# One order of work for the blocks of an expert, lists chosen by masks, at most three blocks unrolled

## The chip, the cores and the metric

The kernel runs on one core of a Trainium2 chip. The metric is the device time of one execution in microseconds (us). Before the change three runs gave a median of 1856.02 us, from 1854.19 to 1857.72. The trace that is read here is one profiled execution of 1859.71 us; the span of its instructions is 1857.6 us.

## What is computed

A decoder layer on 2048 tokens of width 1024 in float32: a mixer (a state-space branch and a convolution branch, gated and projected), a layer norm, a mixture of experts, a layer norm. Only the mixture matters here. Each token is sent to one of 4 groups and to 2 of the 8 experts in that group, 32 experts in all. The rows of an expert are worked in blocks of 128:

```python
def expert_block(args):
    idx, e = args
    xb = xt[idx]
    hid = jax.nn.silu(xb @ w_gate[e]) * (xb @ w_up[e])
    return hid @ w_down[e]
...
y = jax.ops.segment_sum(y_buf.reshape(n_rows, d) * w_buf[:, None], tok_buf, num_segments=n_tok)
```

With the reference's inputs the 32 experts get 11 to 286 rows: 18 experts have one block, 11 have two, 3 have three, 49 blocks together. In order of the experts the blocks are 1 1 1 1 2 1 2 1 2 2 2 1 3 3 2 2 1 1 2 2 1 1 3 1 1 1 2 2 1 1 1 1.

## The kernel before

The mixer and the routing fill the first 1276 us and do not change. Routing writes a table td in DRAM with, for each expert and block, 128 token numbers and weights; cnt holds the counts. The expert stage follows, then the last layer norm on VectorE (from 1798 us on).

Weights are float32 and are split in two parts each, a rounded high part (ScalarE, high) and the rest (VectorE, low); egu holds gate and up of an expert, edn its down matrix. A matmul of float32 precision is three matmuls: high by high, high by low, low by high. Pieces 0 to 3 of an expert's weights are egu, 4 and 5 are edn. The weights of the next expert are split while the present one is multiplied; load and load2 are the DMAs that bring raw weights three experts ahead, on SP's queue.

A block of 128 tokens goes through these steps. gather (Pool, an indirect DMA) brings its rows to a tile. turn transposes them on TensorE in eight pieces (pt), which ScalarE and VectorE split into BH and BL. gateup is 24 matmuls into pg. act makes HID (silu on ScalarE, a product on VectorE). turnh transposes HID in two pieces (ph), split into HH and HL. down is 12 matmuls into pd. emit scales pd by the weights into yy (ScalarE, two halves) and adds it to acc by an indirect DMA of Pool, the scatter. A block is thus 46 matmuls and transposes on TensorE.

On TensorE the steps of neighbouring blocks are interleaved: gateup of a block, turn of the next block, down of the block before, turnh of this block, gateup of the next one. How many blocks an expert has is known only at run time. table(e) loads the count into a register of TensorE, ScalarE, VectorE and Pool (L1369), and each engine branches on it. unit(e, b) is a nest four deep (JB = 4): if the expert has a further block, that block's turn, down, emit, turnh and the next unit follow; if not, the Else holds over(), a copy of the turn of the next expert's first block and the down. So each level has an Else of its own, and an expert of one block jumps over the taken sides of all levels (L1465). The loop over the experts is unrolled.

The rows of a next expert's first block go to XA (two buffers, gathered two experts ahead), those of second and third blocks to XE and XC (gathered by extra, one expert ahead). Which list the last block of an expert has depends on its count; ends copies it by up to four small VectorE copies into IXL and IXQ. BH, BL, HH, HL and HID have two buffers each. Per engine the instructions run in the order of the program; nothing else sets it. After the last expert a count above JB blocks would be worked by a loop (L1524), which does not run here.

Of the kernel before, what the change touches and what calls it, by code (L numbers as in the profile page):

```python
# [10 lines left out]
F32 = mybir.dt.float32  # L11
F32R = mybir.dt.float32r
# [10 lines left out]
S = 2048  # L23
D = 1024
# [4 lines left out]
ALPHA = 2.0 ** 0.25  # L29
EPS = 1e-5  # L30
CAP = 2048
JB = 4
MAGIC = 12582912.0
RSQ = float(0x5F3759DF)

# [50 lines left out]
def layer(ctx, tc, a, out, dbg=None):  # L86
# [1165 lines left out]
    def step(i, *ks):  # L1252
        for k in ks:
            high(i, k)
            low(i, k)
# [6 lines left out]
    for p in range(NP):  # L1262
# [47 lines left out]
        if p == NP - 3:  # L1310
# [27 lines left out]

    ex = ExitStack()
    ep = ex.enter_context(tc.tile_pool(name="ep", bufs=1, side="right"))  # L1340
    XA, XE = [[ep.tile([128, D], F32, name=f"{n}{i}") for i in range(2)] for n in ("xa", "xe")]
    XC = [ep.tile([128, D], F32, name="xc0"),
          wp.tile([128, D], F32, name="xc1", tag="raw", bufs=1, padded_shape=[128, 1024])]
    zero = ident[:, 0:1].to_broadcast([128, D])
    for t in XA:
        A.activation(t, zero, AF.Copy, scale=0.0)
    high(0, 4, 5)
    for t in XE + XC:
        A.activation(t, zero, AF.Copy, scale=0.0)
    high(1, 0, 1)  # L1350

    def pairs(n, name, shape, dt=F32):
        return [ep.tile(shape, dt, name=f"{name}{i}") for i in range(n)]

    BH, BL = [[wp.tile([128, 8, 128], F32R, name=f"{nm}{i}", tag=tag, bufs=2) for i in range(2)]
              for nm, tag in (("bh", "hi"), ("bl", "lo"))]
    HH = pairs(2, "hh", [128, 2, 128], F32R)
    HL = pairs(2, "hl", [128, 2, 128], F32R)
    HID = pairs(2, "hid", [128, FF])
    TAB = ep.tile([128, NE, JB, 2], I32, name="tab")  # L1360
    IXL = pairs(3, "ixl", [128, 2], I32)
    IXQ = pairs(3, "ixq", [128, 2], I32)

    ENG = [ET.PE, ET.Activation, ET.DVE, ET.Pool]
    ALL = ENG + [ET.SP]
    CNT, IX = {}, {}

    def table(e):
        CNT[e] = nc.values_load(cnt[0:1, e:e + 1], engines=ENG, min_val=0, max_val=S)  # L1369
        IX[e] = TAB[:, e]  # L1370

    def lists(e, n):
        A.dma_start(TAB[:, e:e + n].rearrange("p e b c -> p e (b c)"), dap(td, 32 * e, [[1024, 128], [32, n], [1, 2 * JB]]))

    def ends(e, b):

        for t, r in ((IXL[e % 3], IX[e][:, b]), (IXQ[e % 3], IX[e][:, b - 1] if b else IXL[(e - 1) % 3])):
            V.tensor_copy(t[:, 0:1], r[:, 0:1])
            V.tensor_copy(t[:, 1:2].bitcast(F32), r[:, 1:2].bitcast(F32))
            if not e:  # L1380
                break
# [8 lines left out]
    PT = [paux([128, 4, 128], f"pt{i}") for i in range(2)]  # L1390
    PH = paux([128, 2, 128], "ph")

    def turn(xb, i):
        for b in range(2):
            for k in range(4):
                PE.transpose(PT[b][:, k, :], xb[:, (4 * b + k) * 128:(4 * b + k + 1) * 128], ident)
            hi = BH[i][:, 4 * b:4 * b + 4, :]
            A.activation(hi, PT[b], AF.Copy)
            V.tensor_tensor(BL[i][:, 4 * b:4 * b + 4, :], PT[b], hi.bitcast(F32), op=OP.subtract)

    def gateup(i, gu):
        p, hi, lo = PG[i], BH[i], BL[i]
        for k in range(8):
            t = gu[k // 4]
            PE.matmul(p, hi[:, k, :], t[:, 0, k % 4, :], start=k == 0, stop=False)
            PE.matmul(p, hi[:, k, :], t[:, 1, k % 4, :], start=False, stop=False)
            PE.matmul(p, lo[:, k, :], t[:, 0, k % 4, :], start=False, stop=k == 7)

    def act(i, j):
        A.activation(HID[j], PG[i][:, 0:FF], AF.Silu)  # L1410
        V.tensor_tensor(HID[j], HID[j], PG[i][:, FF:2 * FF], op=OP.mult)

    def turnh(j):
        for k in range(2):
            PE.transpose(PH[:, k, :], HID[j][:, 128 * k:128 * k + 128], ident)
        A.activation(HH[j], PH, AF.Copy)  # L1416
        V.tensor_tensor(HL[j], PH, HH[j].bitcast(F32), op=OP.subtract)

    def down(j):
        hh, hl, dn = HH[j], HL[j], DN[j]  # L1420
        for h in range(2):
            c = slice(512 * h, 512 * h + 512)
            for k in range(2):
                PE.matmul(PD[h], hh[:, k, :], dn[:, 0, k, c], start=k == 0, stop=False)
                PE.matmul(PD[h], hh[:, k, :], dn[:, 1, k, c], start=False, stop=False)
                PE.matmul(PD[h], hl[:, k, :], dn[:, 0, k, c], start=False, stop=k == 1)

    def emit(ixc):
        y = ep.tile([128, D], F32, name="yy", bufs=2)
        for h in range(2):  # L1430
            A.activation(y[:, 512 * h:512 * h + 512], PD[h], AF.Copy, scale=ixc[:, 1:2].bitcast(F32))
        G.indirect_dma_start(out=acc, out_offset=bass.IndirectOffsetOnAxis(ap=ixc[:, 0:1], axis=0),
                             in_=y, in_offset=None, bounds_check=S - 1, oob_is_err=False, compute_op=OP.add)

    def unit(e, b):

        i, j = (e + b) % 2, e % 2
        gateup(i, GU[j])
        more = b == 0 and 0 < e < NE - 1
        if more:  # L1440
            step(1 - j, 0, 1, 2)
            high(1 - j, 3)
        if b == 1 and JB > 3:
            with tc.If(CNT[e] > 384):
                gather(XE[j], IX[e][:, 3, 0:1])
        act(i, j)
        if more:
            low(1 - j, 3)
            if e + 3 < NE:
                load(e + 3, 1 - j)  # L1450
        jp, ixp = (j, IX[e][:, b - 1, :]) if b else (1 - j, None)

        def over():
            ends(e, b)
            if e + 1 < NE:
                turn(XA[1 - j], 1 - j)
            if e or b:
                down(jp)
            if b and not e:
                emit(ixp)  # L1460

        if b + 1 == JB:
            over()
            return
        with tc.If(CNT[e] > 128 * (b + 1)) as c:  # L1465
            turn((XE[j], XC[j], XE[j])[b], 1 - i)
            if e or b:
                down(jp)
                emit(ixp if b else IXL[(e - 1) % 3])
            turnh(j)  # L1470
            unit(e, b + 1)
        with c.Else():
            over()

    def extra(e):
        with tc.If(CNT[e] > 128):
            gather(XE[e % 2], IX[e][:, 1, 0:1])
            with tc.If(CNT[e] > 256):
                gather(XC[e % 2], IX[e][:, 2, 0:1])


    low(0, 4, 5)
    load2(2, 0)
    lists(0, 2)
    lists(2, NE - 2)
    high(1, 2, 3, 4, 5)
    low(1, *range(6))
    for e in range(3):
        table(e)
    load(3, 1)  # L1490
    load2(3, 1)
    gather(XA[0], IX[0][:, 0, 0:1])
    gather(XA[1], IX[1][:, 0, 0:1])
    extra(0)
    turn(XA[0], 0)
    for e in range(NE):
        j = e % 2
        if e + 3 < NE:
            table(e + 3)
        if e + 2 < NE:  # L1500
            gather(XA[j], IX[e + 2][:, 0, 0:1])
        if e + 1 < NE:
            extra(e + 1)
        unit(e, 0)
        ahead_ = 0 < e < NE - 1
        if ahead_:
            high(1 - j, 4, 5)
            low(1 - j, 4)
        turnh(j)
        if ahead_:  # L1510
            low(1 - j, 5)
            if e + 3 < NE:
                load2(e + 3, 1 - j)
        if e:
            emit(IXQ[e % 3])
    down((NE - 1) % 2)
    emit(IXL[(NE - 1) % 3])
# [7 lines left out]
    with tc.If(mx > 128 * JB):  # L1525
        with tc.For_i(0, NE, 1) as e:
            c = nc.values_load(cnt[0:1, ds(e, 1)], engines=ALL, min_val=0, max_val=S)
            with tc.If(c > 128 * JB):
                load(e, 0)
                load2(e, 0)  # L1530
                step(0, *range(6))
                with tc.For_i(JB, S // 128, 1) as b:
                    with tc.If(c > b * 128):
                        ix = ep.tile([128, 2], I32, name="ixo", bufs=1)
                        SP.dma_start(ix, td.rearrange("(p e b) c -> e b p c", e=NE, b=S // 128)[ds(e, 1), ds(b, 1)]
                                     .rearrange("e b p c -> p (e b c)"))
                        gather(XA[0], ix[:, 0:1])
                        turn(XA[0], 0)
                        gateup(0, GU[0])
                        act(0, 0)  # L1540
                        turnh(0)
                        down(0)
                        emit(ix)
    ex.close()


# [130 lines left out]
```

## Time and profile before

| What | us |
| --- | --- |
| Median of three runs | 1856.02 |
| Profiled execution | 1859.71 |
| Its span | 1857.6 |
| Expert stage, first gate-up to end of last down | 507.3 |
| TensorE busy in the span | 1712.9 (92%) |
| VectorE busy in the span | 1321.3 (71%) |
| ScalarE busy in the span | 692.6 (37%) |
| Pool busy in the span | 301.1 (16%) |

A row of the timeline gives the start, the length, the engine, the operation with its output and inputs, how many there are, and in brackets how long the engine had been idle and what released it; "issue" means that nothing in the profile explains the wait. Matmuls overlap their neighbours, so a row's length is more than the distance to the next one. The sequencer's rows (a q behind the engine; TensorE's are under PEldq) are register loads, branches and events; they are not counted as busy.

### The profile page before, as it was taken

To read this page: it belongs to the slowest core of one execution; us is meant where nothing else is said; L and a number is where in the kernel's file an instruction comes from. 1 tells how busy PE (TensorE), PEld (TensorE's weight loads), DVE (VectorE), ACT (ScalarE), POOL (GpSimd) and SP (SyncE) were. 2 spreads that over 40 slices of the span, in tenths; PEclk is the share of its full clock that TensorE was granted. 3 is DMA by queue.
4 is the path that set the end of the run, shared out by engine and by line. 5 is a ranking of instruction groups with operands and counts; after the bars stand their busy time and mean duration, and the time that the engine had idled before them with its cause. 6 is when DMAs were issued, how large, how long until landed. Compare 5 with 4: busy or idle time off the path is not lost. (4 is left out here: it accounts for less than half of the span.)

```text
span 1857.6 us, 24068 instructions
## 1 busy us (share of the span) xinstructions
PE 1712.9 (92%) x8360; PEld 1376.4 (74%) x8361; DVE 1321.3 (71%) x2528; ACT 692.6 (37%) x1069; POOL 301.1 (16%) x318
## 2 busy tenths in 40 slices
PE   8999999999999999999999999974899998999940
PEld 7888877777777777877888888853677787877730
DVE  5798787687877884765576678885665556657748
ACT  5111222222222223533321122235665556657744
POOL 2000001101110110000000012212333332323215
PEclk9999999999999999999999999987999999999975
DMA  6321432432342336433553323456888878789755
GB/s 217 92 91 47 121 75 76 141 97 84 97 144 79 97 98 222 121 108 110 185 184 118 143 91 125 171 190 211 266 264 256 269 204 265 220 251 322 231 176 232
DMA packets 213924, 301.40 MB, mean 162 GB/s; under 512 B 29246, under 2 KB 159376, under 8 KB 211168
## 3 DMA queue, kind: packets, MB, share of 16 engines
q1 hardware_dynamic: 166496, 213.32, 35.4%
q0 software_dynamic: 23008, 56.06, 10.9%
q10 hardware_dynamic: 24224, 29.50, 4.7%
q8 instruction: 112, 1.84, 0.4%
q14 instruction: 84, 0.69, 0.1%
HBM read 224.28 MB, written 92.31 MB: 170 GB/s over the span
## 5 line engine op out<-in xcount | busy, mean ns | idle before, releaser
L66 PE MATMUL mm<-xh,whi 128*128 128x512 f32 x896 | 360.8, 403 | 0.0
L66 PE MATMUL mm<-xl,whi 128*128 128x512 f32 x896 | 353.5, 395 | 0.0
L66 PE MATMUL mm<-xh,wlo 128*128 128x512 f32 x896 | 352.2, 393 | 0.0
L66 DVE SCALAR_TENSOR_TENSOR cvw<-cvw,cw 128x1024 f32<-128x1024 f32 x240 | 292.1, 1280 | 0.0
L66 PE MATMUL pg<-egu,bh 128*128 128x512 f32 x784 | 251.5, 402 | 4.7 <-ACT hh L1416 2.8
L66 PEld LDWEIGHTS mm<-xh,whi 128*128 128x128 f32 x896 | 168.3, 188 | 47.9 <-ACT y L712 5.8
L66 PEld LDWEIGHTS mm<-xh,wlo 128*128 128x128 f32 x896 | 168.2, 188 | 41.4
L66 PEld LDWEIGHTS mm<-xl,whi 128*128 128x128 f32 x896 | 168.6, 188 | 36.4 <-issue 0.2
L66 DVE TENSOR_TENSOR egu<-eraw,egu 128x1024 fp32r<-128x1024 f32 x128 | 150.8, 1220 | 33.9 <-ACT egu L1245 33.9
L66 PEld LDWEIGHTS pg<-egu,bh 128*128 128x128 f32 x784 | 145.3, 190 | 37.6 <-ACT hh L1416 3.3
L66 PE MATMUL mm<-yt,whi 128*128 128x512 f32 x512 | 163.8, 401 | 2.0 <-ACT yt L858 1.5
L66 PE MATMUL mm<-wo,mh 128*128 128x512 f32 x512 | 163.6, 401 | 0.0
L66 PE MATMUL pg<-egu,bl 128*128 128x512 f32 x392 | 156.1, 398 | 1.1 <-DVE bl L66 1.1
L731 ACT ACTIVATE gt<-mm,cols 128x512 f32<-128x512 f32 x64 | 44.0, 687 | 265.5 <-PE mm L66 265.5
L66 PE MATMUL pd<-edn,hh 128*128 128x512 f32 x392 | 131.3, 416 | 11.3 <-issue 9.4
L1245 ACT ACTIVATE egu<-eraw 128x1024 fp32r<-128x1024 f32 x128 | 124.9, 1058 | 0.2 <-issue 0.2
L66 PEld LDWEIGHTS mm<-yt,whi 128*128 128x128 f32 x512 | 96.7, 190 | 26.0 <-ACT yt L858 1.5
L66 PEld LDWEIGHTS mm<-wo,mh 128*128 128x128 f32 x512 | 95.0, 190 | 21.8 <-issue 1.2
L66 DVE TENSOR_TENSOR edn<-erd,edn 128x1024 fp32r<-128x1024 f32 x64 | 77.9, 1219 | 38.8 <-ACT edn L1245 38.6
L66 PE MATMUL mm<-yt,wlo 128*128 128x512 f32 x256 | 101.7, 397 | 0.0
L66 PE MATMUL mm<-wo,ml 128*128 128x512 f32 x256 | 101.7, 397 | 0.0
L66 PEld LDWEIGHTS pd<-edn,hh 128*128 128x128 f32 x392 | 72.5, 195 | 27.4 <-issue 11.4
(287 smaller groups left out, 2646.3 us busy)
## 6 DMA issues: line engine op xcount, KB each, us to landing
eraw<-in_w_gate_dram SPq DMA_DIRECT2D x64, 512.0 KB
eraw<-in_w_up_dram SPq DMA_DIRECT2D x64, 512.0 KB
erd<-in_w_down_dram SPq DMA_DIRECT2D x32, 1024.0 KB
gd<-gt ACTq DMA_DIRECT2D x64, 256.0 KB
gl<-gd SPq DMA_DIRECT2D x64, 256.0 KB
wraw<-in_w_in_dram SPq DMA_DIRECT2D x28, 512.0 KB
xt<-in_x_dram SPq DMA_DIRECT2D x16, 512.0 KB
rg<-in_x_dram SPq DMA_DIRECT2D x8, 1024.0 KB
```

Of the source, the lines that this page charges most:

```text
L66: return f(*args, **kw)
L731: A.activation(gt, p, AF.Sigmoid, bias=cols[:, BI + 12 + m:BI + 13 + m])
L1245: A.activation(h, src, AF.Copy)
```

## The change

All blocks follow one order now: gateup and act of a block, turn of the next rows, down of the block before, emit of that block. An expert's first block is outside the If; further(e, b) is one nest of Ifs without Else for the second and third block (JB = 3). For the turn to be the same whatever comes next, select builds two tables once, by masks from the counts (MK: block b exists; OH: block b is the last): NX[e, b] is the list that follows block b of expert e, either of the same expert or the first of the next, LL[e] is list and weights of the last block of e. Where block b is the last, XN holds the next expert's rows. Otherwise XN holds the second block's rows, X1 the third's or the next expert's, X2 the next expert's. XN is gathered one expert ahead, X1 and X2 at the start of the same expert. There is one tile B for both parts of the turned rows, one HH, HL and HID. The copies of ends are gone. emit of the last block stands before the splitting of the next edn (high 4, 5), and those stand before the Ifs.

```diff
-JB = 4
+JB = 3
...
+    for b in range(JB):
+        V.tensor_scalar(MK[:, :, b], pc, 128.0 * b, None, op0=OP.is_gt)
+    V.memset(MK[:, :, 0:1], 1.0)
+    V.tensor_tensor(OH[:, :, 0:JB - 1], MK[:, :, 0:JB - 1], MK[:, :, 1:JB], op=OP.subtract)
+    V.tensor_copy(OH[:, :, JB - 1:JB], MK[:, :, JB - 1:JB])
...
+    def select():
+
+        V.tensor_copy(TF[:, 0:NE], TAB[:, :, :, 0])
+        V.memset(TF[:, NE:NE + 1], float(1 << 20))
+        first = TF[:, 1:NE + 1, 0:1]
+        t = LP[:, :, 0:JB - 1, 0]
+        V.tensor_tensor(t, TF[:, 0:NE, 1:JB], first.to_broadcast([128, NE, JB - 1]), op=OP.subtract)
+        V.tensor_tensor(t, t, MK[:, :, 1:JB], op=OP.mult)
+        V.tensor_tensor(NX[:, :, 0:JB - 1], t, first.to_broadcast([128, NE, JB - 1]), op=OP.add)
+        V.tensor_copy(NX[:, :, JB - 1:JB], first)
+        V.tensor_tensor(LP[:, :, :, 0], TF[:, 0:NE], OH, op=OP.mult)
+        V.tensor_tensor(LP[:, :, :, 1], TAB[:, :, :, 1].bitcast(F32), OH, op=OP.mult)
+        lf = TF[:, 0:NE, 0:2]
+        V.tensor_reduce(lf, LP.rearrange("p e b c -> p e c b"), axis=AX.X, op=OP.add)
+        V.tensor_copy(LL[:, :, 0], lf[:, :, 0])
+        V.tensor_copy(LL[:, :, 1].bitcast(F32), lf[:, :, 1])
...
-    def ends(e, b):
-
-        for t, r in ((IXL[e % 3], IX[e][:, b]), (IXQ[e % 3], IX[e][:, b - 1] if b else IXL[(e - 1) % 3])):
-            V.tensor_copy(t[:, 0:1], r[:, 0:1])
-            V.tensor_copy(t[:, 1:2].bitcast(F32), r[:, 1:2].bitcast(F32))
...
+    def further(e, b):
+
+        j = e % 2
+        with tc.If(CNT[e] > 128 * b):
+            turnh()
+            block(e, b, (e + b) % 2, GU[j])
+            if e + 1 < NE or b + 1 < JB:
+                turn(XB[b])
+            down(j)
+            emit(TAB[:, e, b - 1, 0:1], TAB[:, e, b - 1, 1:2])
+            if b + 1 < JB:
+                further(e, b + 1)
...
+        if e + 2 < NE:
+            table(e + 2)
+        if e + 1 < NE:
+            gather(XN[1 - j], NX[:, e + 1, 0:1])
+        with tc.If(CNT[e] > 128):
+            gather(X1, NX[:, e, 1:2])
...
+        turn(XN[j])
+        if e:
+            down(1 - j)
+            emit_last(e - 1)
+        if more:
+            high(1 - j, 4, 5)
+            low(1 - j, 4)
+        further(e, 1)
+        turnh()
```

TensorE at the end of an expert, before the change: the end of the last Else copy of the down (pd), the branch out of the If, turnh (ph), the load of a count, and the branch for the gathers.

```order
L66 MATMUL pd1_10182<-edn0_10152,hh0_10166 128x512 x2
L66 MATMUL pd1_10182<-edn0_10152,hl0_10168 128x512
L1465 UNCONDITIONAL_BRANCH
L66 MATMUL ph_10185<-ident_69,hid1_10171 128x128 [waits DVE_49]
L66 MATMUL ph_10185<-ident_69,hid1_10171 128x128
L1369 TENSOR_LOAD cnt_5895
L1369 ISA x2
L1476 COMPARE_AND_BRANCH
```

The same place after it, where the matmuls belong to the third block and the two branches with a wait are the skipped sides of the two Ifs.

```order
L66 MATMUL pd1_10178<-edn0_10149,hl_10160 128x512
L1465 UNCONDITIONAL_BRANCH
L1465 UNCONDITIONAL_BRANCH [waits PE_49] x2
L66 MATMUL ph_10181<-ident_69,hid_10161 128x128 [waits DVE_49,PE_49]
L66 MATMUL ph_10181<-ident_69,hid_10161 128x128
L1400 TENSOR_LOAD cnt_5895
L1400 ISA x2
L1497 COMPARE_AND_BRANCH
```

What is new there is the wait of TensorE (PE) on its own count on the skipped side, and that no Else copy stands in its place.

ScalarE at the end of an expert, before the change: the splitting of edn, the high part of turnh (hh), then the scaling of the last block's output (yy).

```order
L1245 ACTIVATE edn1_10194<-erd_9332 128x1024 [waits DMAHW7_49,PE_49]
L1245 ACTIVATE edn1_10194<-erd_9332 128x1024 [waits PE_49]
L1416 ACTIVATE hh0_10166<-ph_10185 128x256 [waits DVE_49,PE_49,Activation_49]
L1431 ACTIVATE yy_11352<-pd0_10181,ixq2_10178 128x512 [waits DMASW7_49,DMASW5_49,DVE_49]
L1431 ACTIVATE yy_11352<-pd1_10182,ixq2_10178 128x512
L1369 TENSOR_LOAD cnt_5895
```

And after it, up to the branch behind which the further blocks or turnh follow.

```order
L1450 ACTIVATE yy_10756<-pd0_10177,ll_10168 128x512 [waits DMASW1_49,DMASW7_49,PE_49,Activation_49]
L1450 ACTIVATE yy_10756<-pd1_10178,ll_10168 128x512 [waits PE_49]
L1245 ACTIVATE edn1_10193<-erd_9332 128x1024 [waits DMAHW7_49]
L1245 ACTIVATE edn1_10193<-erd_9332 128x1024
L1465 COMPARE_AND_BRANCH
L1435 ACTIVATE hh_10159<-ph_10181 128x256 [waits DVE_49,PE_49,Activation_49]
```

The scaling moved ahead of the splitting and of hh.

## Rows read from the trace of the kernel before

**Rows 1.** Page, part 1: busy time, share of the span, instructions of TensorE.

```profile
PE 1712.9 (92%) x8360; PEld 1376.4 (74%) x8361; DVE 1321.3 (71%) x2528; ACT 692.6 (37%) x1069; POOL 301.1 (16%) x318
```

**Rows 2.** Busy time by stretch: us, five engines, granted clock, DMA share, GB/s.

```profile
1278.10:1785.40 507.30, 478.73 (x2247) 384.76 (x2246) 315.35 (x502) 315.20 (x473) 154.46 (x95) 0.98 0.80 243
...
1300.00:1350.00 50.00, 44.14 (x207) 35.43 (x207) 33.62 (x50) 32.99 (x49) 17.04 (x11) 0.97 0.85 265
...
1500.00:1550.00 50.00, 50.00 (x247) 41.09 (x246) 26.39 (x47) 27.75 (x45) 13.22 (x8) 1.00 0.75 209
...
1650.00:1700.00 50.00, 47.18 (x222) 38.14 (x221) 29.80 (x48) 31.05 (x47) 15.26 (x9) 0.97 0.80 234
...
1337.50:1341.00 3.50, 3.50 (x13) 2.91 (x12) 1.38 (x2) 1.19 (x2) 0.00 (x0) 0.51 0.54 119
```

**Rows 3.** Timeline of TensorE: the first transposes, and a clean run of blocks.

```profile
1276.33 1.94 PE L66 MATMUL pt<-ident,xa 128*128 128x128 f32 x8 [21.68 <-DMA xa<-hd,tab]
...
1484.73 0.39 PE L66 MATMUL pd<-edn,hl 128*128 128x512 f32 x1
...
1485.10 0.71 PE L66 MATMUL pg<-egu,bh 128*128 128x512 f32 x2
...
1513.51 0.71 PE L66 MATMUL pg<-egu,bh 128*128 128x512 f32 x2
```

**Rows 4.** TensorE's waits, 1277 to 1786: us in total, times, longest us.

```profile
PE pd L66 <- issue: 9.8, 5, 4.7
PE pt L66 <- issue: 8.9, 7, 2.8
PE pg L66 <- ACT hh L1416: 2.8, 2, 2.2
PE pd L66 <- ACT yy L1431: 1.9, 1, 1.9
PE pg L66 <- ACT edn L1245: 1.7, 5, 0.5
PE ph L66 <- DVE ixl L66: 1.4, 1, 1.4
```

**Rows 5.** Page, part 3: the queue that brings instructions (packets, MB, share).

```profile
q8 instruction: 112, 1.84, 0.4%
```

**Rows 6.** TensorE's sequencer at four places: duration ns min/median/max, first and last start.

```profile
L1465 PEldq COMPARE_BRANCH  x1: 6699/6699/6699, 1308.3 to 1308.3; - x1
...
L1369 PEldq TENSOR_LOAD <-cnt x1: 307/307/307, 1351.3 to 1351.3; - x1
...
L1476 PEldq COMPARE_BRANCH  x1: 233/233/233, 1352.0 to 1352.0; - x1
...
L1369 PEldq TENSOR_LOAD <-cnt x1: 302/302/302, 1384.3 to 1384.3; - x1
...
L1525 PEldq EVENT_SEMAPHORE  x2: 51/51/51, 1785.4 to 1785.6; - x2
```

**Rows 7.** Timeline of TensorE at those four places.

```profile
1315.18 1.07 PE L66 MATMUL pt<-ident,xa 128*128 128x128 f32 x8 [2.52 <-issue]
...
1352.34 0.74 PE L66 MATMUL pg<-egu,bh 128*128 128x512 f32 x2
...
1385.66 0.72 PE L66 MATMUL pg<-egu,bh 128*128 128x512 f32 x2 [0.27 <-ACT edn L1245]
...
1784.97 0.40 PE L66 MATMUL pd<-edn,hl 128*128 128x512 f32 x1
```

**Rows 8.** Groups by form, 1280 to 1780: busy us, mean ns, idle before and releaser.

```profile
L1245 ACT ACTIVATE edn<-erd 128x1024 fp32r<-128x1024 f32 x60 | 60.4, 1053 | 49.1 <-PE pd L66 49.1
```

**Rows 9.** Timeline of Pool: the first gather of the stage.

```profile
1268.21 1.90 POOL L1384 DMA_INDIRECT xa<-hd,tab  x1 [7.28 <-ACT egu L1245]
```

**Rows 10.** The chain that ended last, in order of time: the last two scatters.

```profile
1783.11 1.56 DMA acc<-yy,ixq
...
1788.44 6.23 DMA acc<-yy,ixl
```

More of the change, by code (lines that the diff above doesn't have):

```diff
@@ L1340, in layer, with rowt @@
     ep = ex.enter_context(tc.tile_pool(name="ep", bufs=1, side="right"))
-    XA, XE = [[ep.tile([128, D], F32, name=f"{n}{i}") for i in range(2)] for n in ("xa", "xe")]
-    XC = [ep.tile([128, D], F32, name="xc0"),
-          wp.tile([128, D], F32, name="xc1", tag="raw", bufs=1, padded_shape=[128, 1024])]
+    def rowt(tag):
+        return wp.tile([128, D], F32, name=f"x{tag}", tag=tag, bufs=2, padded_shape=[128, 1024])
+    X1, X2 = rowt("hi"), rowt("lo")
+    XN = [rowt("hi"), rowt("lo")]
@@ L1344, in layer @@
+    XB = [None, X1, X2]
     zero = ident[:, 0:1].to_broadcast([128, D])
-    for t in XA:
-        A.activation(t, zero, AF.Copy, scale=0.0)
+    A.activation(X1, zero, AF.Copy, scale=0.0)
     high(0, 4, 5)
-    for t in XE + XC:
+    for t in XN + [X2]:
         A.activation(t, zero, AF.Copy, scale=0.0)
     high(1, 0, 1)
[L1352 to L1356, printed above, removed]
@@ L1391, in layer, with turn @@
     PH = paux([128, 2, 128], "ph")
-    def turn(xb, i):
+    def turn(xb):
         for b in range(2):
@@ L1396, in turn, with act, turnh @@
                 PE.transpose(PT[b][:, k, :], xb[:, (4 * b + k) * 128:(4 * b + k + 1) * 128], ident)
-            hi = BH[i][:, 4 * b:4 * b + 4, :]
+            hi = B[:, 4 * b:4 * b + 4, 0]
             A.activation(hi, PT[b], AF.Copy)
-            V.tensor_tensor(BL[i][:, 4 * b:4 * b + 4, :], PT[b], hi.bitcast(F32), op=OP.subtract)
+            V.tensor_tensor(B[:, 4 * b:4 * b + 4, 1], PT[b], hi.bitcast(F32), op=OP.subtract)
     def gateup(i, gu):
-        p, hi, lo = PG[i], BH[i], BL[i]
+        p = PG[i]
         for k in range(8):
             t = gu[k // 4]
[L1405 to L1413, printed above, removed]
+            PE.matmul(p, B[:, k, 0], t[:, 0, k % 4, :], start=k == 0, stop=False)
+            PE.matmul(p, B[:, k, 0], t[:, 1, k % 4, :], start=False, stop=False)
+            PE.matmul(p, B[:, k, 1], t[:, 0, k % 4, :], start=False, stop=k == 7)
+    def act(i):
+        A.activation(HID, PG[i][:, 0:FF], AF.Silu)
+        V.tensor_tensor(HID, HID, PG[i][:, FF:2 * FF], op=OP.mult)
+    def turnh():
         for k in range(2):
-            PE.transpose(PH[:, k, :], HID[j][:, 128 * k:128 * k + 128], ident)
-        A.activation(HH[j], PH, AF.Copy)
-        V.tensor_tensor(HL[j], PH, HH[j].bitcast(F32), op=OP.subtract)
+            PE.transpose(PH[:, k, :], HID[:, 128 * k:128 * k + 128], ident)
+        A.activation(HH, PH, AF.Copy)
+        V.tensor_tensor(HL, PH, HH.bitcast(F32), op=OP.subtract)
     def down(j):
-        hh, hl, dn = HH[j], HL[j], DN[j]
+        dn = DN[j]
         for h in range(2):
@@ L1423, in down @@
             for k in range(2):
[L1424 to L1428, printed above, removed]
+                PE.matmul(PD[h], HH[:, k, :], dn[:, 0, k, c], start=k == 0, stop=False)
+                PE.matmul(PD[h], HH[:, k, :], dn[:, 1, k, c], start=False, stop=False)
+                PE.matmul(PD[h], HL[:, k, :], dn[:, 0, k, c], start=False, stop=k == 1)
@@ L1433, in emit, with emit_last, block @@
                              in_=y, in_offset=None, bounds_check=S - 1, oob_is_err=False, compute_op=OP.add)
[L1435 to L1439, printed above, removed]
+    def emit_last(e):
+        emit(LL[:, e, 0:1], LL[:, e, 1:2])
+    def block(e, b, i, gu):
+        gateup(i, gu)
+        act(i)
+    def further(e, b):
[9 more added lines that the diff above has]
+                further(e, b + 1)
@@ new lines, in layer @@
+    low(0, 4, 5)
+    load2(2, 0)
+    lists(0, 2)
+    lists(2, NE - 2)
+    gather(X1, TAB[:, 0, 0, 0:1])
+    high(1, 2, 3, 4, 5)
+    low(1, *range(6))
+    for e in range(2):
+        table(e)
+    load(3, 1)
+    load2(3, 1)
+    select()
+    gather(XN[0], NX[:, 0, 0:1])
+    turn(X1)
+    for e in range(NE):
+        j = e % 2
+        more = 0 < e < NE - 1
+        if e + 2 < NE:
[4 more added lines that the diff above has]
+            gather(X1, NX[:, e, 1:2])
+            if JB > 2:
+                with tc.If(CNT[e] > 256):
+                    gather(X2, NX[:, e, 2:3])
@@ L1442, in unit @@
             high(1 - j, 3)
[L1443 to L1446, printed above, removed]
+        block(e, 0, j, GU[j])
         if more:
@@ L1450, in unit @@
                 load(e + 3, 1 - j)
[L1451 to L1506, printed above, removed]
+        turn(XN[j])
[3 more added lines that the diff above has]
+        if more:
             high(1 - j, 4, 5)
             low(1 - j, 4)
-        turnh(j)
-        if ahead_:
+        further(e, 1)
+        turnh()
+        if more:
             low(1 - j, 5)
@@ L1513, in layer @@
                 load2(e + 3, 1 - j)
-        if e:
-            emit(IXQ[e % 3])
     down((NE - 1) % 2)
-    emit(IXL[(NE - 1) % 3])
+    emit_last(NE - 1)
     g2, b2 = [RAW[1][:, 2 * i:2 * i + 2, :].rearrange("p k c -> p (k c)") for i in range(2)]
@@ L1536, in layer @@
                                      .rearrange("e b p c -> p (e b c)"))
-                        gather(XA[0], ix[:, 0:1])
-                        turn(XA[0], 0)
+                        gather(X1, ix[:, 0:1])
+                        turn(X1)
                         gateup(0, GU[0])
-                        act(0, 0)
-                        turnh(0)
+                        act(0)
+                        turnh()
                         down(0)
-                        emit(ix)
+                        emit(ix[:, 0:1], ix[:, 1:2])
     ex.close()
```

29 lines of the change are left out of this document (16 added, 13 removed).

## The prediction

> **What bounds the kernel now.** The page comes first: TensorE is busy 92% of the span [rows 1], so the question is where it is not. The table of busy time by stretch answers that for the part the change touches. From the first gate-up matmul (1278.10) to the end of the last down matmul (1785.40) run 507.3 us, and in them VectorE and ScalarE are each busy 315 us, TensorE 479; the stretch from 1500 to 1550 is full, the one from 1300 loses 6 us [rows 2]. So TensorE bounds this stage, with holes. The clean rate is read from the TensorE timeline: gate-up starts at 1485.10 and at 1513.51 with two block starts between, 9.47 us a block [rows 3]. The reference's counts make 49 blocks (18 experts with one, 11 with two, 3 with three): 49 x 9.47 = 464. The stage therefore holds about 43 us of loss, and the prediction is a balance of what goes from these 43 and what is put in.
>
> **What the 43 us are.** The list of TensorE's waits [rows 4] names 9.8 us before down matmuls and 8.9 before transposes that no engine or transfer released ("issue", 12 times). A matmul row is 0.40 us long while matmuls follow each other every 0.23, so each such gap is 0.17 longer against the clean rate: 18.7 + 12 x 0.17 = 20.7 us. The sequencer's rows say what they are: the compare-and-branch of L1465, which jumps over the blocks that an expert does not have, once took 6.7 us from 1308.3 [rows 6], and the next transposes on TensorE come at 1315.18 after 2.52 us without work [rows 7]. The queue that brings code moved 112 packets [rows 5]. The order counts 198 matmuls (each with its weight load) between that branch and its target for an expert of one block, 132 for one of two. I read these gaps as waits for code behind a far jump. After the worst of them the clock falls: 1337.5 to 1341 ran at 0.51 [rows 2], a loss of 3.5 x 0.49 = 1.7 us. Five of the ten 50 us stretches show 0.97 [rows 2], each one such fall: 8.5 us. Then waits for data: hh 2.8, the last yy 1.9, ixl 1.4, and 1.7 in five gaps put down to edn, which is long done there [rows 4]; with 0.17 for each gap 9.4. Together 38.6, and some 4.5 in pieces too small to list.
>
> **What the change removes.** The jump becomes 92 matmuls for one block, 46 for two, and an expert's whole code on TensorE 138 instead of 244. I take all 20.7 as gone, since the far jumps are; the bounds are 0 and 20.7. The clock falls go with the gaps that caused them, 8.5. The 32 copies of list ends on VectorE (at most four small ones an expert) go too, with the 1.4 + 0.2 they held up a transpose, and of hh's 3.1 I count all, since VectorE and ScalarE get slack by what follows. Removed: 20.7 + 8.5 + 1.6 + 3.1 + 2.5 (the edn gaps, which the next part counts anew) = 36.4.
>
> [...]
>
> **What the change adds on TensorE.** Before, a skipped block ends in an Else copy of the turn and the down. Now the nested Ifs have no Else, and the order shows on their skipped side a wait of TensorE on TensorE's own count, before turnh. 29 experts take a skipped side (all but the three with three blocks), 28 with a gate-up behind. Until the last down matmul has ended the sequencer reads nothing more; turnh, the register load of the next expert's count, its branches and only then the gate-up follow, where before the sequencer had read them ahead while TensorE still worked. The price, from last down matmul to first gate-up:
> the wait itself: the same kind of wait stands once in before, at the loop's end, where the last down matmul starts at 1784.97 [rows 7] and the event runs at 1785.4 for 0.05 [rows 6]: 0.44 + 0.05;
> leaving the If: 0.07, and issuing two transposes, 0.1;
> load to gate-up: where the sequencer was late in before, the load starts at 1351.3 and gate-up at 1352.34, 1.0 us, with a branch of 0.23 in it; where the next expert has two blocks 1384.3 to 1385.66, 1.36 [rows 6, 7]. For three I take 1.15, between.
> Sum 1.66, against 0.37 in the clean row (1484.73 to 1485.10 [rows 3]): 1.29 lost where the next expert has one block, 1.65 with two, 1.45 with three. With 16, 10 and 2 of these: 20.6 + 16.5 + 2.9 = 40.0, and 0.24 for one more taken branch at each of the 11 two-block experts, 2.6: 42.6. Bounds: 14, if each costs the 0.5 of the longest gap that the load makes today [rows 4]; 76, if each costs the longest fetch gap of transposes, 2.8. I take 42.6 less 1.5, since some of the transposes' time passes under the load: 41.
>
> **The rest.** select and the masks are some 17 small VectorE operations; they lie in the stretch before 1276.33, when TensorE waits 21.7 us for the first gathered rows [rows 3], and I give them 0.5 of delay, between 0 and 2.5. ScalarE now does emit before the two conversions and turnh. The emit waits for the down, as the conversions did (49 us in 30 waits [rows 8]), so nothing new is waited for; hh comes 1.4 us later, but is needed only after a gate-up and a turn (6.4 us). At the last expert no gate-up covers hh: 2 us, in place of the 2.1 for yy. The single B, HH and HID are each read before they are written again in TensorE's own order: nothing. Gathers come one expert ahead, below. The earlier emit of expert 30 lets its scatter land sooner; the last scatter starts at 1788.44 behind the one before it, issued at 1783.11 [rows 10], and I count 1.4 gained, between 0 and 3. Of the 4.5 in small pieces I leave 3.5. SP's loads hang on the same VectorE steps as before. JB = 3 changes nothing for these counts, the largest being 286.
>
> **Sum.** The stage: 464 + 41 + 2 + 3.5 + 0.5 = 511, against 507.3: +3.7; tail -1.4; so +2.3 on the profiled 1859.71 us. That run lies 3.7 above the median, which I take as run-to-run noise; on the median, 1856.02 + 2.3 = 1858.3, rounded to 1858. A difference under 0.2% (3.7 us) can't be told from no change here.
>
> **Rivals.**
> (a) Faster: the wait on its own count is cheap, because the load and branches overlap the end of the down and the transposes more than I think. At 0.5 each (the row of the longest such gap) 14 instead of 41: 1831; at 0.9, 25: 1842. For it: 1.0 from load to gate-up contains a 0.23 branch that is 0.07 when not taken. Against it: a sequencer that stands at a wait can't read on, and 0.44 + 1.0 are both rows of this trace. It decides from 1.1 us each down. 0.27.
> (b) Slower, by the clock: TensorE now has a hole of some 1.3 to 1.9 us per expert with two transposes in it. In before the clock stayed up after the 2.52 gap of 1315.18 (one fall alone in 1300 to 1350, at 1337.5 [rows 2, 7]), so single holes of this size are safe, but not shown for one every 11 us. If the 10 before two-block experts each cost a fall, 10 x 1.7 = 17: 1875. From three falls on this decides. 0.15.
> (c) Slower, by late rows: the second block's rows are gathered at the start of the same expert, behind the XN gather. The first gather of the stage is issued at 1268.21 [rows 9] and its rows are used at 1276.33 [rows 3], 8.1 later. A second one behind it starts some 2 us later, so 10 from the expert's start; turn X1 comes two gate-ups, a turn and a down later, 15 to 16. Pool's queue also holds a scatter that waits for ScalarE's yy. Slack about 3; at DMA shares of 0.85 [rows 2] it can be gone. At 1 us for each of the 14 multi-block experts: 1872. 0.11.
> (d) The change doesn't shorten the waits for code: the gaps have another cause than the jump, or the shorter jump still leaves the code at hand. If half of them stay, 10 + 4 of clock: 1872; if all, 20.7 + 8.5: 1887. For it: 92 matmuls are still a jump, and not each of the 12 gaps can be tied to a long branch. Against it: the 6.7 us branch. 0.10.
>
> **How the numbers follow.** The balance, within 0.2%, has 0.37; (a) 0.27; (b), (c) and (d) together 0.36. The likeliest single case is the balance: 1858. The range reaches into (a) where the wait costs 0.9 and takes (b) to (d) at about their prices: 1842 to 1875; beyond it lie cheap waits (0.1) and two of the slower cases at once (0.08). Since both signs hold much chance: the balance's own range is 1853 to 1862. Faster 0.27, same 0.37, slower 0.36.
>
> **What would show it.** In the profile after: "issue" gaps of 2 to 5 us before transposes and down matmuls gone; in their place, at 28 places, gate-up preceded by 0.9 to 1.5 us of idle TensorE behind turnh, and a TensorE event at L1465 about 0.44 us behind the last down matmul; clock 1.00 in every stretch; the stage's end about 4 us later. Wrong would be: full stretches through one-block experts (a), 0.97 and less in many stretches (b), transposes that wait for gathered rows (c), branches of microseconds (d).

## The result, and the profile after

The changed kernel takes 1942.41 us (median of four runs, 1939.34 to 1944.69) against 1856.87 us for the kernel before (four runs). The ratio is 1.0458, with a 95% interval from 1.0433 to 1.0483: 85 us slower, far outside the range of the prediction. The profiled execution took 1944.69 us.

The page of the changed kernel, part 1 and, from part 3, the queue that brings code (to be held against [rows 1] and [rows 5]):

```profile
PE 1744.2 (90%) x8368; PEld 1393.9 (72%) x8369; DVE 1319.6 (68%) x2421; ACT 706.6 (36%) x1069; POOL 289.2 (15%) x319
...
q8 instruction: 85, 1.39, 0.3%
```

Busy time by stretch, with the columns of [rows 2] (five engines, granted clock, DMA share, GB/s). The first row is the expert stage, from the first gate-up to the end of the last down:

```profile
1281.80:1870.50 588.70, 513.00 (x2255) 406.75 (x2254) 311.43 (x378) 330.26 (x474) 142.76 (x95) 0.92 0.70 207
...
1300.00:1350.00 50.00, 38.48 (x150) 29.80 (x149) 28.72 (x33) 27.78 (x38) 8.97 (x7) 0.83 0.84 245
...
1500.00:1550.00 50.00, 50.00 (x246) 41.26 (x245) 21.10 (x31) 24.90 (x42) 13.10 (x8) 1.00 0.59 156
```

The stage grew from 507.3 to 588.7 us: 81.4 of the 85 are there. It starts 3.7 later (1281.80 against 1278.10). The stretch from 1500 to 1550 is full as before; that is where the experts with two and three blocks lie. So most of the loss sits at experts of one block. What TensorE waits for in the stage, to be held against [rows 4] (us in total, times, longest):

```profile
PE ph L66 <- DVEq L1465: 50.4, 17, 3.0
PE pt L66 <- DMA xhi<-hd,tab: 24.9, 1, 24.9
PE pg L66 <- ACT hh L1435: 17.9, 22, 1.3
PE ph L66 <- PEq L1465: 4.7, 11, 0.4
PE pg L66 <- issue: 1.9, 4, 0.5
PE pd L66 <- ACT hh L1435: 0.8, 1, 0.8
```

The waits before transposes and down matmuls that nothing released, which the prediction read as waits for code, are gone from this list. In their place the transposes of turnh (ph) wait for VectorE's sequencer at the If of the further blocks, 17 times, up to 3.0 us. One such place, in the timeline of all engines, with rows left out:

```profile
1330.51 0.42 DVE L66 TENSOR_TENSOR hid<-hid,pg 128x256 f32<-128x256 f32 x1 [1.81 <-ACT hid L1429]
...
1331.98 1.28 DVE L66 TENSOR_TENSOR bhl<-pt,bhl 128x512 fp32r<-128x512 f32 x2
...
1333.34 0.40 PE L66 MATMUL pd<-edn,hl 128*128 128x512 f32 x1
1333.77 0.69 ACT L1450 ACTIVATE yy<-pd,ll 128x512 f32<-128x512 f32 x1 [0.66 <-PE pd L66]
1334.36 1.99 ACT L1245 ACTIVATE edn<-erd 128x1024 fp32r<-128x1024 f32 x2
...
1335.43 1.23 DVE L66 TENSOR_TENSOR edn<-erd,edn 128x1024 fp32r<-128x1024 f32 x1 [2.17 <-ACT edn L1245]
1336.77 0.69 PE L66 MATMUL ph<-ident,hid 128*128 128x128 f32 x2 [3.04 <-DVEq L1465]
...
1338.39 1.65 PE L66 MATMUL pg<-egu,bhl 128*128 128x512 f32 x3 [0.93 <-ACT hh L1435]
```

And the events of the sequencers at that If, in the same ten microseconds (duration ns min/median/max, first and last start):

```profile
L1465 PEldq EVENT_SEMAPHORE  x1: 51/51/51, 1333.8 to 1333.8; - x1
...
L1465 ACTq EVENT_SEMAPHORE  x1: 17/17/17, 1336.4 to 1336.4; - x1
L1465 DVEq EVENT_SEMAPHORE  x1: 21/21/21, 1336.7 to 1336.7; - x1
```

Read the two together. The last down matmul starts at 1333.34, and TensorE's own wait at the skipped side is over at 1333.8, 0.46 later. HID of this block has been there since VectorE's row of 1330.51 ended at 1330.93. Yet ph starts at 1336.77, right behind VectorE's event at 1336.7. HID is a single tile, and the blocks that are skipped would have written it again; so ph waits for a count of VectorE that contains those writes, and for an expert of one block this count is reached only when VectorE itself passes the skipped If and adds what it left out. VectorE passes it behind low 4, low 4 waits for high 4 on ScalarE, and high 4 stands behind emit, which waits for the down: 3 us.

Counted as in the prediction (0.17 more for each gap than the row says), the loss of the stage over 49 clean blocks (464 us) is 124.7 us:

| Piece | Before | After |
| --- | --- | --- |
| Gaps that nothing released (read as waits for code) | 20.7 | 0 |
| Before turnh: VectorE's pass, 17 times | - | 53.3 |
| Before turnh: TensorE's own wait, 11 times | - | 6.6 |
| Between turnh and gate-up, 26 times (5 before) | 2.6 | 24.2 |
| Half clock | 8.5 | about 39 (what is left) |
| Other data waits, small pieces | 11.3 | 1 |
| Together | 43 | 124.7 |

Half clock in the changed kernel is a granted clock of 0.50, to which it fell at each of the 16 holes of 3.04 us before turnh of one-block experts. Behind the first of them it was 0.50 from 1305.80 to 1312.00, and 1.00 again from 1312.50; the 24 matmuls of the gate-up there took 8.63 us, against 5.81 for those from 1349.95, where the clock was 1.00. The row from 1300 to 1350 shows three such falls (0.83). The 39 is what the other rows leave, not a measurement. The stage's granted clock fits it: 0.92 over 588.7 us is about 94 us at 0.50, which would cost 47 if TensorE had worked through all of them, and part of them lies in holes.

### The profile page after: what moved, and what is told of

It reads as the page before. It is cut to its first block, busy times and chain, and to the rows that moved or that the text cites. A ratio compares the mean times of both kernels' runs of the same rounds, so it can differ in the third digit from the quotient of the medians.

```text
span 1943.0 us, 23915 instructions
## 1 busy us (share of the span) xinstructions
PE 1744.2 (90%) x8368; PEld 1393.9 (72%) x8369; DVE 1319.6 (68%) x2421; ACT 706.6 (36%) x1069; POOL 289.2 (15%) x319
## 3 DMA queue, kind: packets, MB, share of 16 engines
q0 software_dynamic: 23152, 56.06, 11.4%
## 5 line engine op out<-in xcount | busy, mean ns | idle before, releaser
L66 PE MATMUL pg<-egu,bhl 128*128 128x512 f32 x1176 | 320.3, 434 | 19.7 <-ACT hh L1435 17.9
L66 PEld LDWEIGHTS pg<-egu,bhl 128*128 128x128 f32 x1176 | 244.4, 212 | 82.4 <-ACT hh L1435 23.8
L66 PE MATMUL pd<-edn,hh 128*128 128x512 f32 x392 | 126.7, 404 | 0.8 <-ACT hh L1435 0.8
L66 DVE TENSOR_TENSOR hid<-hid,pg 128x256 f32<-128x256 f32 x49 | 20.6, 421 | 131.4 <-ACT hid L1429 131.4
L1451 POOL DMA_INDIRECT acc<-yy,ll x32 | 51.2, 1599 | 276.4 <-ACT yy L1450 254.0
```

The source lines that it names most:

```text
L66: return f(*args, **kw)
```

## The experiments

Theory T: the wait through VectorE's pass of the skipped If makes the holes, and the holes make the clock fall. R1: TensorE's own wait at the skipped side, which the prediction had, is the cost. R2: the clock falls from something else. Each run is told against the changed kernel's 1942.41 us or the run that it builds on; ratios are against the kernel before, run on the same chip. Its medians on these chips went from 1856.9 to 1860.4 us, so where a few us matter, runs of different groups (the first four; the next four; the two after them; the last) are compared by ratio.

### Splitting of the down weights behind the nest of Ifs

```diff
-        if more:
-            high(1 - j, 4, 5)
-            low(1 - j, 4)
         further(e, 1)
+        if more:
+            high(1 - j, 4, 5)
+            low(1 - j, 4)
         turnh()
```

> The changed kernel with the splitting of the next down weights (high 4, 5 and low 4) moved behind the nest of Ifs. Theory T (the wait through VectorE): turnh of a one-block expert waits for VectorE to pass the skipped If, and VectorE gets there only after low 4, which waits for high 4, which waits for emit. With the three behind the nest VectorE passes it early: the 16 holes of 3.20 us before turnh become 0.6 (-42), and the half clock behind them (about 38 us lost) goes: 1942 - 80 = about 1862, 1852 to 1880. Theory R1 (TensorE's own wait at the skipped side is the cost, as predicted): that wait is untouched, 1942. Theory R2 (the clock falls from other causes): only the holes go, about 1900.

Measured: 1861.76 us (ten runs), ratio 1.0021 (1.0012 to 1.0031). The waits of TensorE:

```profile
PE pg L66 <- ACTq L1465: 9.2, 13, 0.9
PE pg L66 <- issue: 7.8, 11, 1.0
PE ph L66 <- DVEq L1465: 6.5, 15, 1.7
PE ph L66 <- PEq L1465: 4.7, 11, 0.4
```

and the stretch that had a clock of 0.83:

```profile
1300.00:1350.00 50.00, 46.40 (x221) 36.51 (x220) 33.84 (x41) 36.12 (x52) 13.72 (x10) 1.00 0.94 288
```

The wait for VectorE's pass fell from 50.4 to 6.5 us, the clock is full (1.00), and the time is T's 1862 to within a microsecond. R1 (1942) and R2 (1900) fall. The stage is again 507.3 us, as long as in the kernel before, in which other things were late.

### Low 4 alone behind the nest

```diff
         if more:
             high(1 - j, 4, 5)
-            low(1 - j, 4)
         further(e, 1)
+        if more:
+            low(1 - j, 4)
         turnh()
```

> The changed kernel with low 4 alone moved behind the nest of Ifs; high 4, 5 stay before it. T: VectorE passes the skipped If early, so turnh starts 0.6 behind the last down matmul; but ScalarE passes it only after high 4, 5 (in the changed kernel 2.6 us behind TensorE), and the next gate-up waits for that pass because of the turned rows, so a hole of about 2.3 us moves from before turnh to before gate-up. Hole per one-block expert about 3 in place of 4.3: -20 to -32, and some of the half clock: 1895 to 1922. If the order of ScalarE alone made the hole: 1942. If only VectorE's pass mattered: as with all three behind, about 1862.

Measured: 1909.78 us (two runs), ratio 1.0275 (1.0254 to 1.0296). The hole moved, as T says, to gate-up, which waits for ScalarE's pass because the skipped blocks would have written the turned rows B:

```profile
PE pg L66 <- ACTq L1465: 34.5, 16, 2.2
```

### Low 5 ahead of the nest as well

```diff
         if more:
             high(1 - j, 4, 5)
-            low(1 - j, 4)
+            low(1 - j, 4, 5)
         further(e, 1)
         turnh()
```

> The changed kernel with low 5 (one more VectorE operation of 1.22 us) moved ahead of the nest of Ifs. T: VectorE passes the skipped If 1.22 us later, 17 times: holes of 4.4 in place of 3.2, +21, and with the clock up to +30: 1960 to 1975. R1: nothing changes, 1942, since the same work is done on an engine that isn't the bound.

Measured: 1963.08 us (two runs), ratio 1.0562 (1.0541 to 1.0583): 20.7 us more for one VectorE operation of 1.22 us that was only moved. The longest wait grew from 3.0 to 4.2 (this list ends before the last of the 17):

```profile
PE ph L66 <- DVEq L1465: 64.4, 16, 4.2
```

This is the dose to the first run's removal: the price of VectorE's lateness is paid in full, one expert after the other.

### The count loaded before the turn

```diff
-        if e + 2 < NE:
-            table(e + 2)
         if e + 1 < NE:
             gather(XN[1 - j], NX[:, e + 1, 0:1])
...
+        if e + 2 < NE:
+            table(e + 2)
         turn(XN[j])
```

> The changed kernel with the load of the count two experts ahead moved from behind turnh to before the turn of the next rows, where TensorE still works. All theories: the 27 pieces between turnh and gate-up (0.58 to 1.50 us, 25.7 in all) fall to about 0.3: -15 to -19, 1923 to 1927, if the load is what fills them. If they are a wait for ScalarE's hh, as the row's releaser says, nothing changes: 1942.

Measured: 1907.62 us (two runs), ratio 1.0263 (1.0243 to 1.0284). The holes before turnh stay (this list begins behind the first of the 17), those before gate-up go:

```profile
PE ph L66 <- DVEq L1465: 48.6, 16, 3.0
PE ph L66 <- PEq L1465: 4.7, 11, 0.4
PE pg L66 <- issue: 1.7, 8, 0.3
```

So the row "pg <- ACT hh" of the changed kernel did not mean that gate-up waits for hh: the register load and its branches filled that time, and hh only ended in it. The gain is 35 us and not 15 to 19. The listed idle fell by 18, so the other half is clock: the clock fell 14 times in place of 16, and it stayed low for about 3.4 us at all of them but one and for about 6.8 there, where the changed kernel had 6.8 at eleven of its sixteen falls.

### Both edits together

> The changed kernel with both edits of the first runs: the splitting of the down weights behind the nest of Ifs, and the load of the count before the turn of the next rows. In the run with the first edit alone the holes between turnh and gate-up sum to 22 us in 26 places (0.65 to 1.15 each). If they are the register load behind TensorE's own wait, they fall to 0.26 to 0.47 each as they did with the second edit alone: -14 to -17 on 1861.8, 1845 to 1848. If ScalarE's pass of the skipped If holds the gate-up there (as half of the rows are labelled), they stay: 1862.

Measured: 1852.61 us (seven runs), ratio 0.9957 (0.9942 to 0.9973), faster than the kernel before. What is left:

```profile
PE ph L66 <- DVEq L1465: 11.4, 15, 1.7
PE ph L66 <- PEq L1465: 4.7, 11, 0.5
PE pg L66 <- issue: 1.4, 7, 0.2
PE pg L66 <- ACTq L1465: 1.1, 5, 0.3
```

Before gate-up 17.6 us went to 2.5 us; 5 us came back before turnh, since VectorE is now closer to TensorE and its pass (behind low 3 and the two parts of the turned rows) is late. The stage takes 495.0 us in place of 507.3: 12 us less, and not the 14 to 17 expected; the time fell by 9, as this run's stage also started 1.6 later. Held against the kernel before on its own chip, it fell from a ratio of 1.0021 to 0.9957, which is 12 us.

### An Else with a copy of turnh

```diff
-        with tc.If(CNT[e] > 128 * b):
+        with tc.If(CNT[e] > 128 * b) as c:
...
             if b + 1 < JB:
                 further(e, b + 1)
+            else:
+                turnh()
+        with c.Else():
+            turnh()
...
-        turnh()
```

In one kernel emit too moves to both sides of the If, behind turnh in the Else; in the other it stays ahead. The splitting of the down weights is behind the nest in both.

> The changed kernel with an Else at each of the two Ifs that holds a copy of turnh and, behind it, of the emit; the splitting of the down weights stands behind the nest. No engine then waits on its own count at a skipped If, and turnh of a one-block expert waits for its own block's HID alone. T: the holes before turnh go (14 us on TensorE's own count and VectorE's in the run with the splitting behind), while gate-up now waits for ScalarE's hh in the Else, which carries the count of the skipped blocks: about 0.6 to 0.75 each in 28 places. Stage 464 + 17 to 21 + 4: 1837 to 1843. If TensorE's waits on its own count cost nothing, the same as with the splitting behind: 1862.

> As the kernel with turnh and emit in the Else, but emit stays ahead of the nest of Ifs, so ScalarE does the two halves of yy (1.37 us) before the hh of the Else. If gate-up waits for that hh, the hole is about 1.4 longer at the 28 experts with a skipped If: 33 us or more slower than the kernel with emit in the Else, 1870 to 1880. If gate-up waits only for the turned rows themselves, the two kernels take the same time.

Measured: 1861.22 us (ten runs), ratio 1.0007 (0.9994 to 1.0020), with emit in the Else, and 1862.24 us (eight runs), ratio 1.0015 (1.0004 to 1.0025), with emit ahead. Both expectations were wrong in size: the first kernel is 20 us slower than expected, and the second equals it. The timeline of the first shows why (a one-block expert):

```profile
1304.42 0.38 PE L66 MATMUL ph<-ident,hid 128*128 128x128 f32 x2
1304.97 0.38 ACT L1435 ACTIVATE hh<-ph 128x256 fp32r<-128x256 f32 x1 [2.46 <-PE ph L66]
...
1305.46 0.42 DVE L66 TENSOR_TENSOR hl<-ph,hh 128x256 fp32r<-128x256 f32 x1 [1.34 <-ACT hh L1435]
1306.03 1.64 PE L66 MATMUL pg<-egu,bhl 128*128 128x512 f32 x6 [1.23 <-ACT yy L1450]
```

ph starts at once, but gate-up starts only 0.15 us behind the end of hl at 1305.88. I read it so: the Else's last VectorE operation, hl, carries the count of the skipped blocks, and the product buffer pg that gate-up writes would have been read in them; so an Else takes away the wait of each engine for itself, and the next user waits for the operation that carries the count. TensorE's list of the second kernel names hl itself at 17 places:

```profile
PE pg L66 <- DVE hl L66: 24.7, 17, 1.5
```

I had looked at ScalarE's part of that (hh, 0.6 to 0.75) and not at VectorE's (hl, about 1.4). With emit ahead only the second half of yy is in hh's way, since the first runs under the down, so the two kernels are alike. The first kernel's releaser, yy, is again only what ended in the gap.

### The kernel before with a nest of three

> The kernel before with JB = 3 and nothing else: the nest is three deep, the jump of a one-block expert passes 132 matmuls in place of 198, that of a two-block expert 66 in place of 132. If the gaps of before that nothing released (20.7 us, and 8.5 us of half clock behind the longest) come from the length of the jump, part of them goes, the shorter ones first: -10 to -29, 1830 to 1848. If they have another cause: 1857.

Measured: 1845.02 us (four runs), ratio 0.9913 (0.9888 to 0.9937). One number was changed, and it is faster than all kernels above. The waits of TensorE:

```profile
PE pt L66 <- DMA xa<-hd,tab: 23.8, 2, 21.9
PE pt L66 <- DMA xe<-hd,tab: 3.6, 2, 1.9
PE pt L66 <- issue: 2.8, 2, 2.3
```

The gaps that nothing released fell from 18.7 us in 12 places [rows 4] to 2.8 in 2, and the queue of code moved 95 packets in place of 112 [rows 5]. That the length of the jump makes these gaps is supported, though the edit also takes away code as such, and the two were not told apart; a branch of this kernel still took 6.4 us, so the long branch itself is not gone, while the longest of these gaps is 2.3 us.

### The late start

> The kernel with both edits (splitting behind, load before the turn), and two zero writes of row tiles ahead of high(0, 4, 5) in place of one, six in all, as the kernel before has them. Theory S (the late start is a collision): with one write fewer ScalarE and VectorE finish the first down weights 1.6 us earlier, so SP's 1 MB load of the next ones starts before the last scatter of the table is issued and the scatter lands 2 us later, which the lists and the first gather wait for. With six writes the first transposes should come after about 22 us of wait as in the kernel before (21.7), not 25: -3, 1849 to 1850. If select or the masks delay the start, the wait stays at 25 and the time at 1852.6.

Measured: 1847.32 us (four runs), ratio 0.9939 (0.9918 to 0.9961). The time is even under the expected one, but not by the mechanism: the first transposes still waited 24.7 us, and the 1 MB load went out at the same moment as the last scatter of the table (rows below). The kernel before was 2.8 us faster on this run's chip too, and the interval overlaps that of the kernel with both edits (0.9942 to 0.9973), so no gain is shown. This run does not test theory S.

```profile
1261.29 0.97 POOL L1206 DMA_INDIRECT td<-r_sd,r_sl  x1 [0.22 <-issue]
...
1261.31 0.37 SPq L1229 DMA_DIRECT2D erd<-in_w_down_dram  x1
```

### Low 3 behind the nest too

```diff
-        if more:
-            low(1 - j, 3)
-            if e + 3 < NE:
-                load(e + 3, 1 - j)
...
         further(e, 1)
         if more:
+            low(1 - j, 3)
+            if e + 3 < NE:
+                load(e + 3, 1 - j)
             high(1 - j, 4, 5)
```

> The kernel with both edits, with low 3 and the load of raw weights behind it moved behind the nest of Ifs too. T: in one-block experts VectorE still passes the skipped If late, because low 3 stands before its two parts of the turned rows: 14 holes before turnh of 0.59 to 1.42 us, 11.8 in all. With low 3 behind they fall to TensorE's own 0.58, or a little over: -3 to -6, 1846 to 1850. Against it: the raw weights are loaded some 3 us later; if the loads are what the next expert waits for, it is slower than 1852.6 by up to that for each one-block expert.

Measured: 1848.33 us (five runs), ratio 0.9944 (0.9923 to 0.9966). Within the expected numbers, yet the hole was mostly moved: VectorE's 11.4 us before turnh fell to 1.7 (and 4.7 beside it that TensorE's own wait makes), while gate-up now waits 7.4 us for ScalarE's pass. The stage is 493.7 against 495.0 us. The rest of the 4 us is an earlier start and is not shown to be the edit's: the kernel before was 2.8 us faster on this chip, and the intervals of the two ratios overlap.

```profile
PE pg L66 <- ACTq L1465: 7.4, 16, 1.5
PE ph L66 <- DVE egu L66: 4.7, 11, 0.4
PE ph L66 <- DVEq L1465: 1.7, 1, 1.7
```

### Lists read ahead of the first down weights

```diff
-    high(0, 4, 5)
...
-    low(0, 4, 5)
-    load2(2, 0)
     lists(0, 2)
     lists(2, NE - 2)
+    high(0, 4, 5)
+    low(0, 4, 5)
+    load2(2, 0)
     gather(X1, TAB[:, 0, 0, 0:1])
```

> The kernel with the splitting behind, the load before the turn and low 3 behind, in which the reading of the lists stands ahead of the splitting of the first down weights, so that SP's 1 MB load of the next ones starts only after the table's scatter has landed (with six zero writes it still started with the last scatter, so that run did not test it). Theory S (the scatter lands late because it shares the transfer with that load): ScalarE's wait for the table falls from 3.5 us to 1.2, the first transposes come 2 to 3 us earlier: 1845 to 1846.5 in place of 1848.3, and about 22.5 us of wait of TensorE in place of 25.2. If the load is not what delays the scatter, the wait stays at 25 and the time at 1848.3 or above.

Measured: 1843.46 us (four runs), ratio 0.9914 (0.9897 to 0.9930). TensorE's wait for the first rows fell from 25.2 us (same kernel without this edit) to 15.0, ScalarE's wait for the table from 4.3 to 2.5. The two runs' rows, without and with the edit:

```profile
PE pt L66 <- DMA xhi<-hd,tab: 25.2, 1, 25.2
...
ACT egu L1245 <- DMA td<-r_sd,r_sl: 4.3, 1, 4.3
```

```profile
PE pt L66 <- DMA xhi<-hd,tab: 15.0, 1, 15.0
...
ACT edn L1245 <- DMA td<-r_sd,r_sl: 2.5, 1, 2.5
```

The start came 10 us earlier and 5 of them arrived at the end: the stage grew from 493.7 to 499.7 us, 3.4 of it one wait of the first gate-up for VectorE's part of the turned rows. The clock has a part in the rest: over the stage's first 20 us it was 0.69, against 0.96 without the edit. The edit moves the reading of the lists and the load at once, so it shows that the order of these steps makes the start late, and not how much of it is the collision.

## Why the prediction was wrong

By its own steps:

- **The step that failed** is the sentence that the single B, HH and HID are each read before they are written again in TensorE's own order, "nothing", and with it "nothing new is waited for" of ScalarE's new order. The data is indeed ready. But a count stands for the data, and on the skipped side that count is raised by VectorE and ScalarE when they pass the If, in their own order. Moving low 4, high 4, 5 and emit ahead of the If put 3 us of other work ahead of that. The holes at that place sum to 53.3 us, of which 9 are left with the splitting behind the nest, and about 39 us of half clock come behind them. The row that says so stood in the order shown with the change: turnh's first transpose waits on VectorE's count. I took it for this block's HID and did not ask which number it waits for.
- **TensorE's own wait**, 41 us, was right in place and size. The event came 0.46 behind the last down matmul's start (0.44 predicted), and where only this wait and what it exposes were left (splitting behind the nest) the holes at the 28 places sum to 38 us: 6.5 + 4.7 + 9.2 + 7.8 in the rows above, 1.1 in two single ones, and what 0.17 a piece adds. That kernel is within 5 us of the 1858 predicted. But 15.7 us of these rows name VectorE's or ScalarE's pass, which the prediction did not have. Before gate-up it is the register load all the same, since moving the load took 17.6 us to 2.5; before turnh, at one-block experts, the share of TensorE's own wait is not shown. The term's upper bound, 76, is a slip: 28 times 2.8 is 78.
- **The waits for code**, 20.7 us, were all gone as predicted. The longest branch of TensorE at that If took 0.36 us in the changed kernel against 6.7 [rows 6]; in runs with the same Ifs single ones took 1.3 (splitting behind), 2.1 (count loaded early) and 2.9 us (both edits), without a gap of that size in TensorE's list. That these gaps are waits for code, and that a jump over 92 matmuls has none where one over 198 has, was my estimate; no run shows what the engine waits for there, or from which length on. Shown is that with 132 and 66 matmuls (the kernel before with a nest of three) 2.8 us in 2 places were left before transposes, and with 92 and 46 (the changed kernel) none before transposes or down matmuls.
- **The clock** was predicted back at 1.00 in every stretch; it was 0.92 in the stage. Rival (b) had falls at holes of 1.9 us before two-block experts. They came at each of the 16 holes of 3.04 us at one-block experts, whether a second hole stood behind turnh (up to 1.34 us, at 14 of them) or none (at the last two). What (b) read out of the kernel before, that single holes of some 2.5 us are safe, its trace does not bear out: one of 2.52 left the clock up, one of 1.93 did not (last section). At the holes that the prediction had priced (0.58 and about 1) no fall was seen.
- **The start**, 0.5 with bounds of 0 and 2.5, was 3.7: the bound was too narrow. What makes the 3.7 stays open: the first gather doesn't use what select makes, and the lists stood behind the first weights before the change too. The last run shows that this order costs more than 3.7 us.
- **The tail**, -1.4, was 0: the last scatter starts 3.1 us behind the end of the last down in both kernels (1873.59 and 1870.50; before [rows 2, 10]).
- Rival (c) (late rows) did not happen: no transfer but the first is in TensorE's list. Rival (d) did not happen.

The range took in single costs that were seen, and had no case in which an engine waits for another one's passing of a branch.

## What to carry to other kernels

Where an If may be skipped, ask for each tile that its body writes or reads: who uses the tile next, and when does each engine that works on it get past the If? In these runs that engine's lateness at the If was on the path of the user, whether or not the data was ready (3.04 us at each of 16 experts in the changed kernel); so work that is not needed by then belongs behind the If, on every engine (the wait for VectorE's pass fell from 50.4 us to 6.5), and what the next step needs from the sequencer (a register load, a branch) ahead of it (the wait before gate-up fell from 17.6 us to 2.5). And before a nest of Ifs is rebuilt for its length, cut the depth that no input uses: that alone gave 0.9% here.

## What the runs showed of the hardware

In this kernel an instruction that waited held up TensorE's sequencer behind it. TensorE's event was done at 1333.8, and the register load behind the two transposes started only at 1336.8, with the transposes:

```profile
L1400 PEldq TENSOR_LOAD <-cnt x1: 584/584/584, 1336.8 to 1336.8; - x1
...
L1400 ACTq TENSOR_LOAD <-cnt x1: 1237/1237/1237, 1337.6 to 1337.6; - x1
...
L1400 DVEq TENSOR_LOAD <-cnt x1: 1198/1198/1198, 1338.0 to 1338.0; - x1
```

So a hole before turnh exposes the load as well. These loads took 0.58, 1.24 and 1.20 us, where three engines load within 1.2 us of each other; most of the others in this kernel took about 0.3 us on each engine. That the nearness makes them slow was not tested.

The granted clock fell at each of the 16 holes of 3.04 us of the changed kernel, and with low 4 behind the nest at each of the 16 holes of 2.15 before gate-up, there for about 3.4 us each. In the kernel with both edits, whose holes were 1.3 us and below but for one of 1.7 at the first expert, it never fell once it had risen early in the stage; with the lists read first it fell behind that same hole of 1.7, which there came 10 us behind one of 3.4. Before the change it fell at five holes of 1.93 to 4.74 us, and one of 2.52 left it up. The first row is the hole of 1.93; the two others are the stretches behind it and behind the one of 2.52, which ended at 1315.18 [rows 7] (columns as in [rows 2]):

```profile
1370.74 0.60 PE L66 MATMUL pt<-ident,xa 128*128 128x128 f32 x4 [1.93 <-issue]
...
1372.00:1374.00 2.00, 2.00 (x6) 1.61 (x5) 0.69 (x1) 0.02 (x1) 0.00 (x0) 0.50 0.07 27
...
1315.00:1317.00 2.00, 1.82 (x12) 1.69 (x13) 2.00 (x7) 1.09 (x2) 0.97 (x1) 1.00 1.06 349
```

So the length of a single hole does not decide in these runs whether the clock falls.
